# Softmax with a temperature on one core: late loads moved to ScalarE's queue, and the last row of the second load cut by partitions

## The chip, the core and the metric

The kernel runs on one core of a Trainium2 chip. Its metric is the device time of one execution in microseconds (us). Five runs of the kernel before give a median of 162.56 us, from 162.36 to 162.7. The profile is of a further execution, with a time of its own.

The engines that matter are VectorE (DVE), ScalarE (ACT), SyncE (SP), and the 16 DMA engines of the core. ScalarE and SyncE also issue DMAs, each through a queue of its own; a queue's DMAs are worked off by all DMA engines.

## The reference

```
x: (16, 1024, 512) float32
x_scaled = x / 2.0
x_max = max(x_scaled, axis=-1)
exp_x = exp(x_scaled - x_max)
out = exp_x / sum(exp_x, axis=-1)        # float32
```

That is a softmax over rows of 512 elements, for 16,384 rows. It reads 33.55 MB from HBM and writes as much.

## The kernel before, in words

The 16,384 rows are 128 partitions times 128 rows. They are cut into twelve tiles, and each tile lies in SBUF as 128 partitions by r rows of 512 floats; every partition's r rows are contiguous in HBM. A tile's rows are worked on in chunks of three to five. The plan gives for each tile its chunks and its place in one arena of 100 rows per partition:

```
PLAN = [
    ([3], 0), ([4, 3], 3), ([5] * 3, 10), ([5] * 3, 25), ([5] * 3, 40), ([5] * 3, 55),
    ([5] * 3, 70), ([5] * 3, 85), ([5] * 3, 10), ([4, 3], 3), ([3], 0), ([3], 25),
]
```

So tile 0 has 3 rows, tile 1 has 7, tiles 2 to 8 have 15, tile 9 has 7, tiles 10 and 11 have 3. The chunks are numbered 0 to 27 through all tiles. Tiles 8, 9, 10 and 11 take the places of tiles 2, 1, 0 and 3. These four are the late loads: the dictionary `behind` holds for each of them the tile whose place it takes, and its load must wait until that tile's store has landed (semaphores `st`).

Work on a chunk k goes through the engines so:

- VectorE takes the negated maximum of each row (`do_max`, line 89), once the tile's load has landed (semaphore `ld`, 16 for one DMA).
- ScalarE computes the exponential of 0.5 times the row plus that bias, in place, with the row's sum as a by-product (line 122), one instruction for each row. It waits for the chunk's maximum.
- VectorE takes the reciprocals of the sums (line 98) and multiplies, again in place: one tensor product over the chunk for tiles 1 to 3 (line 102), one scalar product for each row elsewhere (line 109).

VectorE's order is written out: the maximum of chunk k comes ahead of the multiplication of chunk k - 2 (`LAG = 2`).

All loads of tiles 0 to 7 are issued on ScalarE's queue by `issue_loads` (line 85), those of tiles 0 and 1 ahead of the kernel's opening barrier, the others right after it, ahead of any exponential. Stores are issued on SP's queue (line 145), tile by tile, each when its last chunk is multiplied. The late loads stand on SP's queue too (line 152): tiles 8, 9 and 10 right after the store of tile 4, tile 11 right after the store of tile 5, each after a wait for the store whose place it takes:

```
while late and max(behind[late[0]]) <= t - 2:
    u = late.pop(0)
    for v in behind[u]:
        nc.sync.wait_ge(st[v], 16)
    nc.sync.dma_start(out=sb(u), in_=dram(xf, u)).then_inc(ld[u], 16)
```

GpSimd waits for all stores at the end.

Of the kernel before, what the change touches and what calls it, by code (L numbers as in the profile page):

```python
# [1 line left out]

# [4 lines left out]
# [7 lines that stand above are left out]
]  # L14
ARENA = 100
LAG = 2

FUSED = {1, 2, 3}


@with_exitstack
def kernel(
    ctx: ExitStack,
    tc: tile.TileContext,
    x: bass.AP,
    out: bass.AP,
):
    nc = tc.nc
    fp32 = mybir.dt.float32

    xf = x.flatten_outer_dims()
    of = out.flatten_outer_dims()
    N, D = xf.shape
    P = nc.NUM_PARTITIONS
    n_rows = N // P
    assert sum(sum(c) for c, _ in PLAN) == n_rows

    arena = nc.alloc_sbuf_tensor("arena", (P, ARENA, D), fp32)
    negmax = nc.alloc_sbuf_tensor("negmax", (P, n_rows), fp32)
    sums = nc.alloc_sbuf_tensor("sums", (P, n_rows), fp32)  # L40
    recip = nc.alloc_sbuf_tensor("recip", (P, n_rows), fp32)

    tiles, chunks, base = [], [], 0
    for t, (cs, at) in enumerate(PLAN):
        r = sum(cs)
        tiles.append((base, r, at))
        o = 0
        for c in cs:  # L50
            chunks.append((t, base + o, c, at + o))
            o += c
        base += r
    last_chunk = {c[0]: k for k, c in enumerate(chunks)}

    def dram(ap, t):
        b, r, _ = tiles[t]
        return ap[b * P : (b + r) * P].rearrange("(p r) d -> p r d", r=r)

    def sb(t):  # L60
        _, r, at = tiles[t]
        return arena[:, at : at + r, :]


    behind = {}
    for t, (_, r, at) in enumerate(tiles):
        for u in range(t):
            _, ru, au = tiles[u]
            if at < au + ru and au < at + r:
                behind.setdefault(t, []).append(u)  # L70

    ld = [tc.alloc_semaphore(f"ld{t}") for t in range(len(tiles))]
    awaited = sorted({u for us in behind.values() for u in us})
    st = {t: tc.alloc_semaphore(f"st{t}") for t in awaited}
    s_end = tc.alloc_semaphore("s_end")
    s_max = tc.alloc_semaphore("s_max")
    s_exp = tc.alloc_semaphore("s_exp")
    s_rec = tc.alloc_semaphore("s_rec")
    s_mul = tc.alloc_semaphore("s_mul")

    def issue_loads(begin, end):

        for t in range(begin, end):
            if t not in behind:
                nc.scalar.dma_start(out=sb(t), in_=dram(xf, t)).then_inc(ld[t], 16)

    def do_max(k):
        t, b, c, a = chunks[k]
        nc.vector.reduce_max(  # L89
            out=negmax[:, b : b + c],  # L90
            in_=arena[:, a : a + c],
            axis=mybir.AxisListType.X,
            negate=True,
        )._wait_ge(ld[t], 16).then_inc(s_max, 1)

    def do_mul(k):
        t, b, c, a = chunks[k]
        nc.vector.reciprocal(  # L98
            out=recip[:, b : b + c], in_=sums[:, b : b + c]
        )._wait_ge(s_exp, k + 1).then_inc(s_rec, 1)  # L100
        if t in FUSED:
            nc.vector.tensor_mul(  # L102
                out=arena[:, a : a + c],
                in0=arena[:, a : a + c],
                in1=recip[:, b : b + c].unsqueeze(2).to_broadcast([P, c, D]),
            )._wait_ge(s_rec, k + 1).then_inc(s_mul, 1)
            return
        for r in range(c):
            ins = nc.vector.tensor_scalar_mul(  # L109
                out=arena[:, a + r],  # L110
                in0=arena[:, a + r],
                scalar1=recip[:, b + r : b + r + 1],
            )
            if r == 0:
                ins._wait_ge(s_rec, k + 1)
        ins.then_inc(s_mul, 1)

    def compute_and_store():

        for k, (t, b, c, a) in enumerate(chunks):  # L120
            for r in range(c):
                ins = nc.scalar.activation(  # L122
                    out=arena[:, a + r],
                    in_=arena[:, a + r],
                    func=mybir.ActivationFunctionType.Exp,
                    bias=negmax[:, b + r : b + r + 1],
                    scale=0.5,
                    accum_out=sums[:, b + r : b + r + 1],
                )
                if r == 0:  # L130
                    ins._wait_ge(s_max, k + 1)
            ins.then_inc(s_exp, 1)


        for k in range(len(chunks) + LAG):
            if k < len(chunks):
                do_max(k)
            if k >= LAG:
                do_mul(k - LAG)


        late = sorted(behind)
        for t in range(len(tiles)):
            nc.sync.wait_ge(s_mul, last_chunk[t] + 1)
            nc.sync.dma_start(out=dram(of, t), in_=sb(t)).then_inc(
                st[t] if t in awaited else s_end, 16
            )
            while late and max(behind[late[0]]) <= t - 2:
                u = late.pop(0)
                for v in behind[u]:  # L150
                    nc.sync.wait_ge(st[v], 16)
                nc.sync.dma_start(out=sb(u), in_=dram(xf, u)).then_inc(ld[u], 16)

        for t in awaited:
            nc.gpsimd.wait_ge(st[t], 16)
        nc.gpsimd.wait_ge(s_end, 16 * (len(tiles) - len(awaited)))

    hook = nc.inst_callbacks[-1]  # L160
    nc.remove_inst_callback(hook)
    symbolic = nc._always_lower_symbolic_ap
    nc._always_lower_symbolic_ap = False
    here = str(nc.cur_bb)
    entry = nc.main_func.blocks[0]
    head, jumps = entry.instructions[:-5], entry.instructions[-5:]
    entry.instructions = []
    nc.switch_bb("main", None)
    issue_loads(0, 2)
    first = list(entry.instructions)  # L170
    at = next(k for k, i in enumerate(head) if type(i).__name__ == "InstDrain")
    entry.instructions = head[:at] + first + head[at:]
    issue_loads(2, len(tiles))
    compute_and_store()
    entry.instructions = list(entry.instructions) + jumps
    nc.switch_bb(here, None)
    nc._always_lower_symbolic_ap = symbolic
    nc.push_inst_callback(hook)


# [1 line left out]
_INS = ['x']  # L182
_OUTS = [((16, 1024, 512), 'float32')]


# [23 lines left out]
```

## Time and profile before

| | |
|---|---|
| median of 5 runs | 162.56 us (162.36 to 162.7) |
| profiled execution, its own time | 162.3 us |
| its span, first to last instruction | 160.5 us |
| VectorE busy | 131.7 us, 82% of the span |
| ScalarE busy | 94.6 us, 59% |
| moved by DMA | 67.13 MB, mean 418 GB/s |
| HBM read, written | 33.55 MB, 33.55 MB |

The page of a profile has busy times of the engines; the span in 40 equal slices, with a digit for the busy tenths of each; the DMA queues with packets, megabytes and the time of their packets as a share of the 16 engines' span; and the chain of work that ended last. Other views give instructions in order of time, waits, and the busy times in chosen stretches. In lists in order of time the first number is the start in us from the beginning of the span, the second the duration. ACTq and SPq are the DMA issues of ScalarE and SyncE. The trace has also a record of each DMA packet (start, size, duration, queue, but not which of the 16 engines) and, for each DMA, the times at which its semaphore was raised, sixteen to a DMA.

DMA issues by line, with their size and the median time to landing, are these: seven stores of 3840 KB on SP's queue take 21.7 us from issue to landing; six loads of that size on ScalarE's queue 46.9 us; one on SP's queue 29.7 us; and the load of tile 1 (1792 KB) 8.2 us.

### The profile page before, as it was taken

Reading aid. Unit: us, or ns where it says so; the run is one execution under the profiler, and the core shown is the slowest. Engines: PE = TensorE matmul, PEld = TensorE weight load, DVE = VectorE, ACT = ScalarE, POOL = GpSimd, SP = SyncE. Lnnn points to the kernel's source line nnn. Section 1 sums busy time; section 2 is a strip of 40 time slices with the busy share of each in tenths; the row PEclk is TensorE's granted clock in tenths of the full one; section 3 lists DMA queues with packets and bytes.
Section 4 is the critical chain, followed back from the end, with each engine's and each line's share of the span. In section 5 each row is a group of like instructions: output and inputs, shape, how many; then the busy total and the mean of one; then the engine's idle time right before and its main releaser. Section 6 shows DMA issues by size and latency. Waiting matters only on the chain.

```text
span 160.5 us, 480 instructions
## 1 busy us (share of the span) xinstructions
DVE 131.7 (82%) x155; ACT 94.6 (59%) x257; POOL 0.2 (0%) x4
## 2 busy tenths in 40 slices
DVE  0485599999999999999999999999999999970000
ACT  0739076759547746866679766688666875630000
POOL 0000000000000000000000000000000000000000
DMA  7999999999999999999998999999999999999994
GB/s 292 453 398 467 404 410 403 387 473 390 432 452 406 459 421 436 444 413 469 390 475 383 475 390 461 413 411 443 450 413 441 436 421 475 390 467 398 413 407 167
DMA packets 3459, 67.13 MB, mean 418 GB/s; under 512 B 384, under 2 KB 384, under 8 KB 1152
## 3 DMA queue, kind: packets, MB, share of 16 engines
q1 hardware_dynamic: 2304, 40.90, 59.4%
q10 hardware_dynamic: 1152, 26.21, 38.8%
q14 instruction: 3, 0.02, 0.0%
HBM read 33.55 MB, written 33.55 MB: 418 GB/s over the span
## 4 chain that ended last, share of the span: by engine, by line
DVE 78%; DMA 10%; issue 0%; DVEq 0%
DVE negmax L89 40%; DVE arena L109 23%; DVE arena L102 13%; DMA arena<-in_x_dram 10%; DVE recip L98 2%; DVEq L204 0%
## 5 line engine op out<-in xcount | busy, mean ns | idle before, releaser
L122 ACT ACTIVATE arena<-arena,negmax 128x512 f32<-128x512 f32 x128 | 90.8, 710 | 42.6 <-DVE negmax L89 42.6
L89 DVE TENSOR_REDUCE negmax<-arena 128x5 f32<-128x2560 f32 (+2 forms) x28 | 72.3, 2584 | 10.9 <-DMA arena<-in_x_dram 10.9
L109 DVE TENSOR_SCALAR arena<-arena,recip 128x512 f32<-128x512 f32 x91 | 37.8, 482 | 0.7
L122 ACT ACTIVATION_READ_ACCUMULATOR arena<-arena,negmax 128x1 f32 x128 | 23.9, 187 | 0.0
L102 DVE TENSOR_TENSOR arena<-arena,recip 128x2560 f32<-128x2560 f32 (+2 forms) x8 | 21.0, 2624 | 0.3
L98 DVE RECIPROCAL recip<-sums 128x5 f32<-128x5 f32 (+2 forms) x28 | 4.9, 175 | 0.0
L122 ACT ACT_TABLE_LOAD x1 | 1.3, 1283 | 4.5 <-issue 4.5
L193 POOL MEMSET const-bfloat16-1.0<- 128x1 bf16 x1 | 0.1, 101 | 0.0
L193 POOL MEMSET const-uint8-127<- 128x1 uint8 x1 | 0.1, 101 | 0.0
L193 POOL MEMSET const-float32-1.0<- 128x1 f32 x1 | 0.1, 99 | 0.0
L193 POOL MEMSET const-float32-0.0<- 128x1 f32 x1 | 0.1, 98 | 0.2 <-issue 0.2
## 6 DMA issues: line engine op xcount, KB each, us to landing
out_dram<-arena SPq DMA_DIRECT2D x7, 3840.0 KB, 21.7
arena<-in_x_dram ACTq DMA_DIRECT2D x6, 3840.0 KB, 46.9
arena<-in_x_dram SPq DMA_DIRECT2D x1, 3840.0 KB, 29.7
out_dram<-arena SPq DMA_DIRECT2D x2, 1792.0 KB, 16.3
out_dram<-arena SPq DMA_DIRECT2D x3, 768.0 KB, 15.4
arena<-in_x_dram ACTq DMA_DIRECT2D x1, 1792.0 KB, 8.2
arena<-in_x_dram SPq DMA_DIRECT2D x1, 1792.0 KB, 33.5
arena<-in_x_dram SPq DMA_DIRECT2D x2, 768.0 KB, 33.7
```

Of the source, the lines that this page charges most:

```text
L89: nc.vector.reduce_max(out=negmax[:, b : b + c], in_=arena[:, a : a + c], axis=mybir.AxisListType.X, negate=True,)._wait_ge(ld[t], 16).the ...
L98: nc.vector.reciprocal(out=recip[:, b : b + c], in_=sums[:, b : b + c])._wait_ge(s_exp, k + 1).then_inc(s_rec, 1)
L102: nc.vector.tensor_mul(out=arena[:, a : a + c], in0=arena[:, a : a + c], in1=recip[:, b : b + c].unsqueeze(2).to_broadcast([P, c, D]),)._w ...
L109: ins = nc.vector.tensor_scalar_mul(out=arena[:, a + r], in0=arena[:, a + r], scalar1=recip[:, b + r : b + r + 1],)
L122: ins = nc.scalar.activation(out=arena[:, a + r], in_=arena[:, a + r], func=mybir.ActivationFunctionType.Exp, bias=negmax[:, b + r : b + r ...
L193: nc = _bacc.Bacc("TRN2", target_bir_lowering=False, num_devices=1)
```

## The change

Two things change. First, the late loads are issued by ScalarE, between the exponentials: those of tiles 8, 9 and 10 after the last exponential of tile 4, that of tile 11 after the last one of tile 6. ScalarE waits there for the stores whose places they take. SP is left with stores alone.

Second, tile 1's load is three DMAs on ScalarE's queue rather than one: its first six rows over all 128 partitions, its seventh row over partitions 0 to 125, and the seventh row over partitions 126 and 127. The maximum waits for 48 rather than 16.

```diff
+AFTER = {8: 4, 9: 4, 10: 4, 11: 6}
+
+SPREAD = 1
...
         for t in range(begin, end):
-            if t not in behind:
+            if t == SPREAD:
+
+                r = tiles[t][1] - 1
+                for p, q, lo, hi in ((0, P, 0, r), (0, 126, r, r + 1), (126, P, r, r + 1)):
+                    nc.scalar.dma_start(
+                        out=sb(t)[p:q, lo:hi], in_=dram(xf, t)[p:q, lo:hi]
+                    ).then_inc(ld[t], 16)
+            elif t not in behind:
                 nc.scalar.dma_start(out=sb(t), in_=dram(xf, t)).then_inc(ld[t], 16)
...
-        )._wait_ge(ld[t], 16).then_inc(s_max, 1)
+        )._wait_ge(ld[t], 48 if t == SPREAD else 16).then_inc(s_max, 1)
...
+        late = sorted(behind)
         for k, (t, b, c, a) in enumerate(chunks):
+            while late and last_chunk[AFTER[late[0]]] < k:
+                u = late.pop(0)
+                for v in behind[u]:
+                    nc.scalar.wait_ge(st[v], 16)
+                nc.scalar.dma_start(out=sb(u), in_=dram(xf, u)).then_inc(ld[u], 16)
...
-        late = sorted(behind)
         for t in range(len(tiles)):
             nc.sync.wait_ge(s_mul, last_chunk[t] + 1)
             nc.sync.dma_start(out=dram(of, t), in_=sb(t)).then_inc(
                 st[t] if t in awaited else s_end, 16
             )
-            while late and max(behind[late[0]]) <= t - 2:
-                u = late.pop(0)
-                for v in behind[u]:
-                    nc.sync.wait_ge(st[v], 16)
-                nc.sync.dma_start(out=sb(u), in_=dram(xf, u)).then_inc(ld[u], 16)
```

Neither the arithmetic nor the order on VectorE changes.

## The prediction

> **What bounds the kernel now.** I read the page first: engines' busy time, slices, DMA queues.
>
> ```profile
> DVE 131.7 (82%) x155; ACT 94.6 (59%) x257; POOL 0.2 (0%) x4
> ...
> DVE  0485599999999999999999999999999999970000
> ACT  0739076759547746866679766688666875630000
> ...
> DMA  7999999999999999999998999999999999999994
> GB/s 292 453 398 467 404 410 403 387 473 390 432 452 406 459 421 436 444 413 469 390 475 383 475 390 461 413 411 443 450 413 441 436 421 475 390 467 398 413 407 167
> ...
> q1 hardware_dynamic: 2304, 40.90, 59.4%
> q10 hardware_dynamic: 1152, 26.21, 38.8%
> ```
>
> VectorE has the larger share of any compute engine, but stops four slices before the end; the DMA row is full from the second slice to the last but one. The two queues (q1 is SP's, q10 ScalarE's, by their bytes) took 98.2% of the 16 DMA engines' time: 157.6 of 160.5 us. The chain is no guide here. It follows VectorE to its end, and after that only stores run:
>
> ```profile
> 142.33 0.49 DVE arena L109
> 142.82 0.40 DVEq L204
> 143.22 0.40 DVE arena L109
> ```
>
> The last store is issued at 143.64 us (timeline) and lands at 159.44 (the last of its sixteen completions in the trace). So about 15 us of transfers are queued when the last multiply ends, and the end is the time at which the slowest DMA engine has worked off its share. The stretches say whether two active queues move data faster than one:
>
> ```profile
> 50.00:75.00 25.00, 24.82 (x24) 16.28 (x45) 0.00 (x0) 1.00 1.00 433
> 75.00:93.00 18.00, 17.89 (x27) 14.12 (x40) 0.00 (x0) 1.00 1.00 430
> 93.00:127.00 34.00, 33.75 (x50) 24.97 (x70) 0.00 (x0) 1.00 1.00 430
> 127.00:143.00 16.00, 15.79 (x32) 10.13 (x28) 0.00 (x0) 1.00 1.01 434
> ```
>
> Before 93 us loads (ScalarE's queue) and stores (SP's) share the engines; after it everything is in SP's queue. The last columns are DMA share and GB/s: 433, 430, 430, 434. It makes no difference.
>
> **The engines are not even.** The sixteen completions of the last store in the trace: ten at 158.06 to 158.34, then 158.65, 158.75, 158.91, 158.99, and two at 159.42 and 159.44. Followed packet by packet (each starts within 5 ns of the previous one's end on its engine), fourteen engines begin the first load at 1.15 to 1.39 us, two at about 2.02 and 2.10. The first load's completions show the same: the last two at 4.50 and 4.53, the other fourteen at 3.50 to 4.15. A pair lags from the start, by about 0.7 us, and by 1.1 at the end. The mean of the last store's completions is 158.5, so a perfect balance is worth 0.9 us.
>
> **The change, part by part.** First, the split of tile 1's load. Packet records of the trace: 30,720 bytes take 1138 ns, 14,336 take 535, 6,144 take 234. The slope from the smallest to the largest is 27.2 bytes per ns, with 8 ns on top. So 12,288 bytes are an estimated 460 ns, 2,048 an estimated 83; a completion packet takes 9. Every DMA of this trace gives each engine 8 data packets and a completion (128 and 16 packets). Before, tile 1 costs an engine 8 x 535 + 9 = 4289 ns. After, the six-row part costs 8 x 460 + 9 = 3689. The seventh row's 126 partitions are no multiple of 16; the nearest rows show equal shares only, and the largest equal division is 14 x 9. Then fourteen engines pay 9 x 83 + 9 = 756 more: 4445, which is +0.16 us. Two engines get none of it: -0.60 us. The last two partitions put one packet on each of two engines, +0.09 there, or +0.25 in all. Which engines are left out no row shows. If shares are dealt in order and the pair that begins last is last in that order, it is the pair. Then the pair ends at 159.44 - 0.60 = 158.84, the next engines at 158.99 + 0.16 = 159.15, and 159.15 is the new end: -0.29 us. If the pair is not left out: +0.16 to +0.25. So between -0.6 (no more can come off the pair) and +0.25; I take the order of beginning, the only row there is.
>
> The median, 162.56, is 0.26 above the profiled execution's 162.3 (span 160.5 and 1.8 around it). Nothing shows where a usual run spends that; if it is on the pair, up to 0.55 can come off. So the forecast from the median is 162.27 down to 162.01; I take 162.2, nearer to the end that rests on rows, a gain of 0.36.
>
> The Trainium skill speaks against it twice. "DMA: Bandwidth & Descriptors", Latency and other measured facts, says that DMA engines 7 and 15 are usually the slow ones, and with equal shares dealt from the lowest number, as its section on why a semaphore goes up by 16 has it, 7 would be among the fourteen: 159.44 + 0.16, or 162.7. The trace has no engine numbers. Its Rules for kernel authors also hold that a transfer cut by partitions gains nothing over one of 128.
>
> Second, the two added issues. ScalarE's eight issues in this profile end at 4.51 us, 0.33 to 0.60 each, and the table load follows:
>
> ```profile
> 0.13 4.38 ACTq L85 DMA_DIRECT2D arena<-in_x_dram  x8
> 4.54 1.28 ACT L122 ACT_TABLE_LOAD   x1 [4.54 <-issue]
> 6.34 0.72 ACT L122 ACTIVATE arena<-arena,negmax 128x512 f32<-128x512 f32 x1 [0.52 <-DVE negmax L89]
> ```
>
> Two more are about 1.1 us; 0.52 of it lies in the wait before the first exponential, so this chunk's exponentials end 0.6 later, near 9.1. They are wanted by the reciprocal at 12.67: 3.5 us of cover; without it 0.6 us would go to a VectorE that has 15 us to spare. Tile 2's issue goes from 1.41 to about 2.5; its ring holds tiles 0 and 1 until 8 us. Nothing.
>
> Third, the late loads. SP loses four issues and its waits on stores; stores 5 and on no longer stand behind loads in a ring. ScalarE gets the issues of tiles 8, 9, 10 ahead of tile 5's exponentials, at 68.4, and that of tile 11 ahead of tile 7's, at 97.8. The waits are over by then: the stores of tiles 2, 1, 0 have landed by 66.63, that of tile 3 by 85.2. Queued behind them are the exponentials, which idle anyway:
>
> ```profile
> 67.58 0.71 ACT L122 ACTIVATE arena<-arena,negmax 128x512 f32<-128x512 f32 x1
> 68.19 0.19 ACT L122 ACTIVATION_READ_ACCUMULATOR arena<-arena,negmax 128x1 f32 x1
> 69.66 0.72 ACT L122 ACTIVATE arena<-arena,negmax 128x512 f32<-128x512 f32 x1 [1.29 <-DVE negmax L89]
> ```
>
> Three issues are 1.57 us on SP; 1.29 is idle, 0.3 us is made up in the next chunk's 1.29. If store 2 landed later than 68.4, VectorE would notice only after 5.8 us (its reciprocal for that chunk is at 79.48, the exponentials end at 73.3).
>
> Tile 8 then shares the engines with store 5 rather than following store 4 alone. Its 8 packets per engine take 2 x 8 x 1.138 = 18.2 us from 91.3 (most engines) or 93.3 (the pair), so it lands at 109.5 to 111.5, against 106.9 now; its maximum starts at 111.26. A stall of 0.3 us at most, under the 7 us by which store 8 is issued (134.3) ahead of its turn in the ring (141). Tiles 9 to 11 follow at about 120, 124, 127; they are wanted at 126, 134, 138. Bytes and packets per engine are as before and no engine runs dry, so this part is 0: between -0.1 (all that the packets after 75 us take beyond 1138, 535 and 234, per engine) and +0.3.
>
> **Rivals.** First, slower: the row of 126 partitions lands on fewer engines than fourteen. Place: tile 1's ring; price: 126/n packets of 83 ns less 600 on each of n engines. It decides once an ordinary engine, ending at 158.99, passes 159.44, which is at 13 packets, fewer than ten engines. On seven it is 18 x 83 - 600 = 0.9 on top of 158.99: +0.45, 163.0. On two, 63 x 83 - 600 = 4.6: +4.2, 166.8. For it: no transfer of this trace has other than sixteen shares. Against: the sixteen are always equal, and 126 divides by fourteen. Chance 0.10.
>
> Second: the pair is among the fourteen. +0.16 to +0.25: 162.7 to 162.8, which a measurement of this kernel (about 0.2%, 0.33 us) can hardly tell from no change; 0.25. For it: the order of beginning may be that of HBM, not of numbers. Against: two out of sixteen late together fits a remainder of the same kind.
>
> Third: the late loads starve VectorE, so that DMA engines run dry near the end. The stall must pass 7 us; with 5 us more than that lost, 167. Only if the load of tile 8 waits for something that I do not see. 0.03.
>
> **How the numbers follow.** Forecast 0.62: 162.2, own range 161.85 to 162.4; faster by over 0.2% (below 162.23) in 0.50, within in 0.12. Second rival: within in 0.16, slower in 0.09 (162.9 and over, if small packets cost more than the slope). First and third: slower, 0.12, with 0.01 within. Sum: faster 0.50, same 0.29, slower 0.21. The range 161.8 to 162.95 holds the forecast and most of the second rival and leaves out the rest.
>
> **What would show it.** In the profile after: 2,048-byte packets, 83 ns; two of sixteen engines without any; the last store's two latest completions within 0.4 us of the others rather than 1.1 behind ten of them; late loads in ScalarE's queue with 430 GB/s throughout; no wait of the maximum on loads after 18 us beyond 0.3 at tile 8. Wrong, if the last two completions stay 1.1 us behind, or a few engines carry the row, or the DMA row has a gap after 100 us.

## The result, and the profile after

The changed kernel takes 162.11 us in the median of 45 runs (161.87 to 162.75), the kernel before 162.55 in 85 runs (161.92 to 163.37). The ratio is 0.9972, with a 95% interval of 0.9964 to 0.9979: about 0.45 us less. The forecast was 162.2. The number was right; the experiments show that the reason was not.

The page after (engines' busy time, slices, DMA queues; q10 is ScalarE's queue, q1 SP's):

```profile
DVE 131.9 (82%) x155; ACT 94.5 (59%) x257; POOL 0.2 (0%) x4
...
DVE  0466499999999999999999999999999999506800
ACT  0629176768448646766688666797666875501300
...
DMA  7998999998999999999999999999999999999994
...
q10 hardware_dynamic: 1872, 33.56, 49.5%
q1 hardware_dynamic: 1728, 33.56, 48.7%
```

The DMA row is as full as before, and each queue now carries one direction. But VectorE has a hole near the end that it did not have, and finishes two slices later. Waits of VectorE, and the chain (start, duration, what) near the end, say why:

```profile
DVE negmax L100 <- DMA arena<-in_x_dram: 18.8, 5, 7.4
```

```profile
138.37 7.35 another core or an unknown queue
145.72 0.02 issue
145.75 1.75 DVE negmax L100
```

Before, VectorE waited for loads 10.9 us in three waits, the last of which ended at 18.03:

```profile
DVE negmax L89 <- DMA arena<-in_x_dram: 10.9, 3, 4.5
```

Now there are two more, 0.3 us for tile 10 and 7.4 us for tile 11 (the profile calls the load an unknown queue in the chain). The late loads land at 110.6, 123.9, 134.8 and 145.7 us, against 106.9, 111.2, 113.3 and 124.2. The last three stores are issued late:

```profile
148.92 3.13 SPq L161 DMA_DIRECT2D out_dram<-arena  x3
```

The DMA engines are still behind by then (by the packet records all sixteen are at work until 157 us), so it costs nothing.

In the packet records a second thing is gone. Late in the kernel nearly all packets of one size take the same time to some 20 ns, so one that takes much longer has been stalled. From 105 us on, before and after (start in us, ns too long, bytes):

```
before:  111.40 +146 6144 | 111.50 +151 6144 | 111.78 +250 6144 | 111.88 +165 6144
after:   nothing over 36 ns
```

The four stalled packets belong to the load of tile 10, which runs alone on SP's queue when ScalarE's is empty. The loads of tiles 8, 9 and 11 run alone there too, and in this profile have no such packet but one, which follows an instruction fetch (98.17 us, +244; a fetch is a packet of 8,192 bytes on a third queue). Ahead of 105 us the changed kernel is not free of stalls either: at 87.55 a packet of tile 7's load, beside stores, takes 337 ns too long.

A stall makes one DMA engine late, and the latest engine sets the time: in all fourteen profiles of this document, the execution's time is the latest completion of the last store plus 2.84 to 2.86 us. That completion is 1.1 us behind the median of the sixteen in the kernel before (1.3 in its second profile), and 0.9 in the changed kernel.

### The profile page after: what moved, and what is told of

Same layout as the page of the kernel before. It is cut to its first block, busy times and chain, and to the rows that moved or that the text cites. A ratio compares the mean times of both kernels' runs of the same rounds, so it can differ in the third digit from the quotient of the medians.

```text
span 160.3 us, 482 instructions
## 1 busy us (share of the span) xinstructions
DVE 131.9 (82%) x155; ACT 94.5 (59%) x257; POOL 0.2 (0%) x4
## 4 chain that ended last, share of the span: by engine, by line
DVE 78%; DMA 10%; another core or an unknown queue 5%; issue 0%; DVEq 0%
DVE negmax L100 40%; DVE arena L120 23%; DVE arena L113 13%; DMA arena<-in_x_dram 10%; DVE recip L109 2%; DVEq L215 0%
```

## The experiments

All runs are compared with the kernel before on the same chip; a ratio has its 95% interval. "Latest" and "median" are those of the last store's sixteen completions.

### Each part alone

The cut alone: `issue_loads` and the wait as in the change, late loads on SP's queue as before.

```diff
+            if t == SPREAD:
+                r = tiles[t][1] - 1
+                for p, q, lo, hi in ((0, P, 0, r), (0, 126, r, r + 1), (126, P, r, r + 1)):
...
-        )._wait_ge(ld[t], 16).then_inc(s_max, 1)
+        )._wait_ge(ld[t], 48 if t == SPREAD else 16).then_inc(s_max, 1)
```

> Only tile 1's load is cut (six rows, then 126 and 2 partitions of the seventh); the late loads stay on SP's queue. Theory A (the two late DMA engines are relieved of 0.60 us): the whole gain is here, ratio to the kernel before 0.997 to 0.998, the last store's two latest completions no longer about 1 us behind the others. Theory B (the gain is the late loads' new queue): 1.000 to 1.001.

Measured: 163.38 against 162.83, ratio 1.0026 (1.0006 to 1.0047). Slower.

The late loads alone (the edit is against the changed kernel):

```diff
-SPREAD = 1
+SPREAD = None
```

> Only the late loads move to ScalarE's queue; tile 1's load is one DMA. Theory A: 1.000, with the pair still about 1 us behind at the last store. Theory B: 0.997 to 0.998. Both: tiles 9, 10 and 11 land at about 124, 135 and 146 us as with the whole change, and the last store is issued near 152.

Measured: 162.22 against 162.83, ratio 0.9964 (0.9944 to 0.9984). The whole gain is the late loads' move, and the cut adds nothing to it. Theory A, that of the prediction, has fallen.

The latest of the last store's completions is at 160.57 with the cut alone, though no pair stands apart any more (at tile 2's landing the two latest are 0.18 and 0.32 us behind the median; 0.63 and 0.63 before). The records show what holds the end instead:

```
cut alone: 111.95 +307 6144 | 122.72 +735 6144 | 122.81 +412 6144 | 123.69 +184 6144
late only: nothing over 44 ns
```

With the cut alone, the latest engine is 1.07 us behind the median at the landing of tile 10's load, and 2.04 behind at that of tile 11's, which holds the packet of +735 ns; at the last store it is 2.08. In the DMA row from 157 to 161 us, 0.1 us to a digit, it is the thin tail past 159, one engine at work (a single engine is 0 or 1):

```profile
DMA  8898999798132120202011010101010000000000
```

In the run of the late loads alone, all sixteen last completions lie between 159.03 and 159.21. That is not because no engine was late: store 9 is issued at 149.75, when the first engines have finished store 8, and all of them start it in step. The stretches show the engines run dry (last columns: DMA share, GB/s):

```profile
148.00:150.00 2.00, 1.93 (x7) 1.64 (x5) 0.00 (x0) 1.00 0.75 323
150.00:152.00 2.00, 1.97 (x6) 0.58 (x2) 0.00 (x0) 1.00 0.82 344
```

### Two other cuts

The seventh row of tile 1 as one DMA over 128 partitions (the maximum then waits for 32), and as DMAs over 120 and 8; the late loads stay on SP's queue. The edit is against the cut alone.

```diff
-                for p, q, lo, hi in ((0, P, 0, r), (0, 126, r, r + 1), (126, P, r, r + 1)):
+                for p, q, lo, hi in ((0, P, 0, r), (0, P, r, r + 1)):                        # the one
+                for p, q, lo, hi in ((0, P, 0, r), (0, 120, r, r + 1), (120, P, r, r + 1)):  # the other
```

> Late loads on SP's queue; tile 1's seventh row is a DMA of its own, over all 128 partitions, so that no engine is left out. Theory A: each engine pays 8 x 460 + 9 + 8 x 83 + 9 = 4362 ns rather than 4289, +0.07 us, ratio 1.000 to 1.001, the pair still last. Theory C (what helps is cutting the second load, or issuing the later ones later, whichever engines carry it): 0.997 to 0.998.

Measured: 0.9996 (0.9973 to 1.0018).

> Late loads on SP's queue; the seventh row is cut into 120 and 8 partitions. Theory A with equal shares dealt in a fixed order of engines: 120 is 15 x 8, so one engine is left out, the seventh row's semaphore gets 15 completions, one of the pair comes 0.66 us earlier and the other stays last: ratio 0.999 to 1.001. If the pair lies elsewhere in the order, neither moves. Theory C: 0.997 to 0.998.

Measured: 1.0019 (0.9999 to 1.0038). Theory C's 0.997 to 0.998 is ruled out by this cut; the interval of the one over 128 partitions still reaches it. The largest stalls after 105 us were 451 and 487 ns, again in 6,144-byte load packets.

### Which late loads, and when

Only tiles 10 and 11 on ScalarE's queue; SP keeps tiles 8 and 9 where they were, with the old loop over those two. The edit is against the changed kernel, with `SPREAD = None`:

```diff
+ON_ACT = {10, 11}
...
-        late = sorted(behind)
+        late = sorted(t for t in behind if t in ON_ACT)
```

> Only the two small late loads (tiles 10 and 11, packets of 6,144 bytes) move to ScalarE's queue; tiles 8 and 9 stay on SP's, tile 1's load is one DMA. Theory D (small load packets that run with nothing from the other queue between them stall single engines by 0.15 to 0.75 us at 111 and 122 us): the stalls above 50 ns after 110 us go, ratio 0.996 to 0.998, and the last store is still issued near 144 us. Theory E (the gain comes with the big late loads, tiles 8 and 9, on ScalarE's queue): 0.999 to 1.001.

Measured: 162.30 against 162.74, ratio 0.9968 (0.9954 to 0.9982), last store issued at 143.9. Moving two loads of 768 KB gives as much as moving all four, within the intervals. But the stalls did not all go: two, of 326 and 413 ns, are in the load of tile 9, 14,336-byte packets, which now runs alone after tile 11's has landed at 112.2. The profiled execution, 162.40 us, was also no faster than that of the kernel before, 162.3; so it does not show where the gain of the median comes from.

The mirror image: `ON_ACT = {8, 9}`, with tiles 10 and 11 behind SP's store of tile 6 (against the run just above):

```diff
-            while late_sp and max(behind[late_sp[0]]) <= t - 2:
+            while late_sp and t == 6:
```

> The other half: tiles 8 and 9 on ScalarE's queue, while tiles 10 and 11 stand on SP's queue behind the store of tile 6, so that they run alone at about 130 to 134 us; tile 1's load is one DMA. Theory D: stalls of 0.15 us and more on single engines at 130 to 134 us, ratio 0.999 to 1.002. Theory E: 0.996 to 0.998, and no such stalls.

Measured: 163.01, ratio 1.0015 (1.0001 to 1.0029). There are 16 stalls of 0.1 us or more, at 130.3 to 132.5, the largest +864 and +850, and the latest completion is at 160.43. The stalls have moved with the small loads, and the gain is lost though the big loads are on the new queue. Theory E falls.

The two small loads moved, and the cut with them (`SPREAD = 1`):

> Tiles 10 and 11 on ScalarE's queue and tile 1's load cut as in the change. If relieving the pair of late engines by 0.6 us is worth something once the stalls are gone: 0.3 us below the run with the two small loads alone, ratio 0.994 to 0.996. If the cut costs by itself (as it did without the late loads' move): above that run by 0.2 to 0.6 us.

Measured: 162.27 against 162.74, ratio 0.9973 (0.9962 to 0.9983), where the move alone had 0.9968. With the small loads on ScalarE's queue the cut neither gains nor costs anything that can be told.

### Packet size, or running alone

The last two tiles as one of six rows, on SP's queue:

```diff
-    ([5] * 3, 70), ([5] * 3, 85), ([5] * 3, 10), ([4, 3], 3), ([3], 0), ([3], 25),
+    ([5] * 3, 70), ([5] * 3, 85), ([5] * 3, 10), ([4, 3], 3), ([3, 3], 25),
```

> The kernel before with its last two tiles (3 rows each) made one tile of 6 rows, whose load of 12,288-byte packets stands on SP's queue behind the store of tile 5 and runs alone near 121 to 125 us. If it takes small packets to stall an engine: no stall above 0.15 us after 110 us, ratio 0.996 to 0.998. If any late load that runs alone does it: one or more stalls of 0.15 us and above there, ratio 0.999 to 1.001.

Measured: 163.01 against 162.67, ratio 1.0012 (0.9994 to 1.003). Packets twice the size stall as badly: at 121.1 to 123.5, up to +838, +795 and +758 ns. The size of the packet is not what does it.

No late load alone: `ON_ACT = {8, 10, 11}`, tile 9 on SP's queue behind the store of tile 3, where the old rule of `behind` puts it.

> Tiles 8, 10 and 11 load on ScalarE's queue, tile 9 on SP's behind the store of tile 3, so that it runs beside tile 7's load near 85 to 95 us; tile 1's load is one DMA. No late load then runs with the other queue empty. If that is what counts: no stalls above 0.15 us after 80 us but the one that goes with each instruction fetch, ratio 0.996 to 0.998, and the last store issued near 144 us. If two loads beside each other stall as one alone does: stalls at 85 to 95 us, ratio 0.999 to 1.001.

Measured: 162.09 against 162.67, ratio 0.9958 (0.9942 to 0.9974), the lowest of all, though its interval overlaps that of the change. After 80 us one packet is over by more than 36 ns, by 180, and it follows an instruction fetch. VectorE's waits are as before the change:

```profile
DVE negmax L101 <- DMA arena<-in_x_dram: 11.0, 3, 4.6
```

Tile 9's load runs on SP's queue beside loads of tiles 7 and 8 here, and does not stall (9 ns at most). So in this profile a load on SP's queue with another load beside it did not do what such loads did with the other queue empty. What both queues did from 110 to 135 us, first in the kernel before, then in this one:

```profile
q1 hardware_dynamic: 623, 10.88, 101.6%
```

```profile
q1 hardware_dynamic: 358, 9.52, 88.4%
q10 hardware_dynamic: 229, 1.21, 11.6%
```

The same window from 157 to 161 us, first for the small loads run alone on SP's queue at 130 us, then for the merged tile, then with no load alone, and last for the kernel before:

```profile
DMA  9799999947144241212211020110100000000000
```

```profile
DMA  8299595580550225020250222220000000000000
```

```profile
DMA  9998949598814205030000000000000000000000
```

```profile
DMA  9597998744241220202000000000000000000000
```

In the first two, one to four engines go on to 159.6 us and later while the others stand idle; in the third the row ends by 159. So does that of the kernel before, whose profiled execution, 162.3 us, was one of its faster ones: what no load alone gains on it there is little, 0.1 us, and the gain of 0.42% is in the medians.

### Second profiles, and one that went elsewhere

> The kernel before once more, for a second profile of its stalls after 110 us: one to four packets of 6,144 bytes 0.15 us or more too long at 111 to 112 or 122 to 124 us, as in the first, and a last completion that stands with the largest of them.

> The cut of tile 1 alone once more, for a second profile. If the cut costs because the engines then run closer in step and collide more: again a stall of 0.4 us or more at 111 to 124 us, larger than in the second profile of the kernel before. If the two first profiles differed by chance: stalls of the same size as there.

The kernel before had three stalls of 0.1 us or more in tile 10's and 11's loads again (268, 231 and 141 ns) and a fourth at 122.85 of 100, and one of 720 ns at 98.81, in the load of tile 8, also alone; its latest completion was at 159.61. The cut alone had ten after 105 us, of 315 ns at most, and ended at 161.04 (163.90 us in all). So the second pair does not show larger stalls with the cut, but more of them; one engine was 1.67 us behind at tile 8's landing already. That the engines collide more for being in step is not shown.

Tile 9 row by row, in the whole change:

```diff
+                if u == 9:
+                    for r in range(tiles[u][1]):
+                        nc.scalar.dma_start(
+                            out=sb(u)[:, r : r + 1], in_=dram(xf, u)[:, r : r + 1]
+                        ).then_inc(ld[u], 16)
```

> The whole change, but tile 9's load is seven DMAs of one row (2,048 bytes to a packet). If two queues take turns by packet: each small packet waits for a store packet of 1138 ns, 56 of them would need 68 us, so tile 9 lands only when SP's stores have run out (145 us or later rather than 124), VectorE stands still and the time rises by 2 to 5 us. If they share by bytes, as the prediction counted (tile 9 at about 120): tile 9 lands where it did, and the time stays within 0.3 us.

Measured: 180.61 in two runs, ratio 1.1097 (1.1075 to 1.112). It does not decide what it was meant to, since ScalarE itself stood still. Issues in order of time, and the wait:

```profile
69.11 15.11 ACTq L139 DMA_DIRECT2D arena<-in_x_dram  x5
84.26 16.09 ACTq L143 DMA_DIRECT2D arena<-in_x_dram  x1
```

```profile
ACT arena L145 <- issue: 31.6, 1, 31.6
```

One of tile 9's issues and the next tile's took 11.7 and 16.1 us rather than 0.5, with the exponentials queued behind them; SP's stores ran out meanwhile. The question was answered by the profile after: tile 9's load takes 123.9 - 110.6 = 13.3 us there, and 8 x (535 + 1138) ns are 13.4; tiles 10 and 11 take 10.9 each, and 8 x (234 + 1138) are 11.0. At both sizes the queues take turns packet by packet.

This run shows something else that bears on the stalls. From 102 to 113 us SP's queue is empty, and what is left of tile 8's load and the loads of tiles 9 and 10 run alone on ScalarE's queue, 1072 packets, none more than 19 ns too long. At 125.8, on the other hand, a store beside tile 11's load has a packet 368 to 846 ns too long on every one of the sixteen engines. So a load that runs alone does not always stall, and company does not always help. The loads that did stall alone after 105 us were all on SP's queue, behind stores; whether it takes that queue as well as the emptiness of the other was not tested.

## Why the prediction was right in the number and wrong in the reason

**What bounds the kernel**: right. The end is that of the slowest DMA engine, 2.84 to 2.86 us ahead of the execution's time in every profile, and in the changed kernel neither ScalarE's two added issues nor VectorE's wait of 7.4 us moved it.

**The cut, its mechanism**: right. Tile 1's semaphore is raised by 16, 14 and 2 completions, and twice at issue for the shares that are not there. Packets of 2,048 and 12,288 bytes take 84 and 460 ns. The two engines that begin last, at 2.08 and 2.09 us, carry no 2,048-byte packet. Of the two places of the Trainium skill that the prediction set against this, the one on engines 7 and 15 ("DMA: Bandwidth & Descriptors", Latency and other measured facts) is called there specific to DMAs that GpSimd issues, of which this kernel has none; the other, that a cut by partitions gains nothing, agrees with the cut alone, 1.0026.

**The cut, its worth**: wrong. The step that failed is "the pair ends at 159.44 - 0.60, the next engines at 158.99 + 0.16, and 159.15 is the new end". It took one execution's lags for the kernel's. Of the pair's 1.1 us, some 0.3 came from the stalls at 111 us: the two latest completions are 0.75 and 0.81 us behind the median at tile 9's landing and 1.06 and 1.09 at tile 10's. In another execution such stalls can fall on other engines. Where a stalled engine among the fourteen sets the end, the cut gives it 0.16 to 0.25 us more and nothing back: 0.10 to 0.15% of the time, inside the interval of the cut alone. That is argued; the second profile of the cut alone, with one engine far behind at tile 8 already, says that it need not be all.

**The late loads**: wrong, and the largest error. The sum had 0, with -0.1 as its lower end: "all that the packets after 75 us take beyond 1138, 535 and 234, per engine". That is a mean over sixteen engines, put in for a quantity that is a maximum. The packets of +146 to +250 ns stood in the records of before. Measured alone: 0.36% of 162.55, or -0.59 us (-0.26 to -0.91). That the two errors, -0.36 for the cut and 0 for the loads, add up to nearly the right total is luck. The measured parts do not add up to the whole: +0.26% and -0.36% against -0.28% together; with the loads moved the cut's cost does not show, and why is open.

**The stretches**: the mean rates of 430 to 434 GB/s were read as "it makes no difference" which queue carries what. They hold after the change as well:

```profile
75.00:93.00 18.00, 17.89 (x27) 14.12 (x39) 0.00 (x0) 1.00 1.01 434
93.00:127.00 34.00, 33.75 (x50) 24.96 (x71) 0.00 (x0) 1.00 1.01 434
127.00:143.00 16.00, 10.97 (x20) 8.13 (x23) 0.00 (x0) 1.00 0.99 427
```

The one that is lower, 427, is from the faster kernel. A stall of 0.3 us on one engine is 0.02 us in the mean of sixteen, and cannot be seen there.

**The signs**: the 2,048-byte packets of 84 ns and the two engines without them came as foretold. The last store's two latest completions, 158.99 and 159.27, are 0.6 and 0.9 us behind the median, not within 0.4 us of the others; and VectorE's wait for a load after 18 us was 7.4 us at tile 11, not 0.3 at tile 8. The right number hid both.

**When the late loads land**: wrong. "About 120, 124, 127" for tiles 9 to 11 shared the engines by bytes; by packets it is 123.9, 134.8 and 145.7. The third rival came close: its stall of over 7 us happened (7.7 us in two waits), though for the turns of the queues and not at tile 8. Store 9 was issued at 140.84 before, 9 us ahead of its turn, and is issued at 148.92 now, 1.2 us ahead of the first engine that asks for it at 150.1. With the late loads alone this cover was gone, and the engines ran dry.

**ScalarE's issues**: right. They end at 69.2 us, and the next exponential still idles 1.29 us before it starts at 69.89.

**The rivals**: the row did land on fourteen engines, and the pair was left out, so the first two fell. None of them had a gain from the queue.

## What to carry to other kernels

Where sixteen DMA engines set the end, look at the latest of a transfer's completions and at single packets that take too long, not at the bandwidth of a stretch. Which queue carries a late load is worth an experiment even where the mean rate says that it makes no difference: here two loads of 768 KB moved to the other queue gave 0.3%. A rule for it these runs do not give: on SP's queue with ScalarE's empty, late loads cost up to 0.86 us on single engines, but not each time. Before two queues are mixed, count what each gets by packets and not by bytes, and see how much cover is left for what waits on the queue with the small packets.

## What the runs showed of the hardware that was not expected

Late loads on SP's queue with nothing on ScalarE's stalled single packets by 0.1 to 0.86 us, at 6,144, 12,288, 14,336 and 30,720 bytes, though not every such load did; stores alone did not (29 ns at most from 127 us on in the kernel before). It is no rule of loads that run alone: 1072 packets alone on ScalarE's queue were clean, and beside stores single load packets stalled too, by 337 ns at 87.55 in the changed kernel and by up to 373 ns near 39.9 us in the kernel before. Why is open: the records do not say where a packet waits.

Issues on ScalarE's queue took 11.7 and 16.1 us with several transfers already queued there, and ScalarE's computing stood still for it.

Two of the sixteen engines begin the first load 0.7 us after the others, and are the two that a DMA over 126 partitions leaves out. Taking 0.6 us off them with the cut gained nothing that could be told, alone (1.0026) or with the small loads moved (0.9973 against 0.9968).
